# Column tiles of a projection in pairs by seven half-size products, in a hybrid attention block on one Trainium2 core

## The chip, the cores and the metric

The kernel runs on one core of a Trainium2 chip. The metric is device time in microseconds (us) of one launch. TensorE (PE) multiplies, VectorE (DVE) and ScalarE (ACT) work elementwise, GpSimd (POOL) fills, issues DMAs and does small things, SyncE (SP) issues the loads. Each engine works through its own queue in a fixed order and waits there on semaphores.

## The reference

One layer on 512 tokens of width 2048, in float32:

```python
h = rms_norm(x, pre_norm_w)
proj = h @ w_in   # sb_q | sb_k | sb_v | sb_gate | mla_c_q | mla_c_kv | mla_k_rope | mla_gate
...
y = concat(o_A * silu(sb_gate), o_B * silu(mla_gate)) @ w_out
return x + rms_norm(y, post_norm_w)
```

o_A is stick-breaking attention: 8 heads of 128, with weights sigmoid(z) times the running product of 1 - sigmoid(z) over the later keys. o_B is latent attention: 8 heads with low-rank queries and keys, a rotary part and a softmax.

## The kernel before, in words

**Numbers in two parts.** Every float32 operand is kept as a high and a low part in the type float32r (split, L94): ScalarE writes the rounded high part, VectorE the rest. One product is three matmuls (mm3, L127): high by high, high by low, low by high.

**Tiles.** hh and hl hold h transposed: 16 tiles of [128 columns of the model, 512 tokens]. column_proj (L217) makes one tile of 128 projected columns, [column, token]: two loads of weights of 512 KB each (weights, L104: one [128, 1024] tile raw, its parts whi and wlo), and for each 8 products on 512 tokens, 48 matmuls in all, in one PSUM bank. sb_queries (L360) and sb_keys (L367) make a head's q and k so, gate (L339) a head's gate; the per-token factor rstd_bc comes in afterwards. group_proj (L189) makes the values, four heads at a time, token by column.

**Order.** TensorE runs what is traced, in that order. The projections stand in a generator, filler (L449), that yields after each product; fill(n) (L467) takes n of its steps and stands between the parts of attention, so that TensorE has work while the other engines do softmax or scans. The filler makes the latents, eight gates, and then for every stick-breaking head its q, k and gate, with the values of four heads ahead of heads 0 and 4; then the output projection. The other engines' queues are ordered by the framework's scheduler; loads go out from SP in the order of the program.

**A stick-breaking head** (L733 to L760): four blocks of scores z, each masked on VectorE, two sigmoids on ScalarE (keep and beta), a scan (prod) and a product on VectorE; then, for each block of keys, transposes tp, their parts th and tl, and a product av with the values (Weighted, L576). The result is multiplied with the gate (mix) and put aside in memory.

**Buffers.** The pool ring holds raw in N_RAW = 2 slots and whi and wlo in N_HI = 3 each. A tile that takes a slot again waits until the last reader of the tile before it is done. One pool, gen, holds everything else for the whole run.

Of the kernel before, what the change touches and what calls it, by code (L numbers as in the profile page):

```python
# [10 lines left out]
F32 = mybir.dt.float32  # L11
# [46 lines left out]
def block(ctx: ExitStack, tc: tile.TileContext, a: dict):  # L58
# [4 lines left out]
    gen = ctx.enter_context(tc.tile_pool(name="gen", bufs=1))  # L63
    dram = ctx.enter_context(tc.tile_pool(name="dram", bufs=1, space=bass.MemoryType.DRAM))
# [4 lines left out]
    def g(name, dt=F32, tag="g"):  # L69
        return gen.tile([P, S], dt, tag=tag, name=name, bufs=SLOTS[tag])  # L70

# [40 lines left out]
    def small_weights(src, n, pin=False):  # L112
        raw = ring.tile([P, 768], F32, tag="mraw", name="mraw", bufs=1)
# [6 lines left out]
    # TensorE runs what is traced, in that order: the order below keeps it fed.  # L120
# [31 lines left out]
    def rms_factor(name, ss, n, cols):  # L152
        """(ss / n + eps) ** -0.5"""
# [6 lines left out]
    # TensorE's clock rises while it works  # L160
# [11 lines left out]
    def load_h(k, cuts=(slice(0, S),)):  # L172
        xk = g(f"xt{k}")
        hi, lo = g(f"hh{k}", F32R), g(f"hl{k}", F32R)
# [42 lines left out]
    def column_proj(t, out):  # L217
        """One tile of 128 columns, transposed: [column, token]; yields after each product."""
# [33 lines left out]
    def turns(n, unit, name):  # L252
        """fraction of a turn in n * unit radians, n a whole number of at most 12 bits"""
# [34 lines left out]
    # [block, half, 32]: cosines twice; sines with the sign of their half; the queries' ones scaled  # L288
    tabs = {}
    for nm, s in (("k", 1.0), ("q", MLA_SCALE)):  # L290
        ct = const.tile([P, NB, 2, 32], F32, name="cos_" + nm)
        st = const.tile([P, NB, 2, 32], F32, name="sin_" + nm)
# [19 lines left out]
    def latent(banks, n, width, name):  # L312
        """The scaled projection, token-major, and the sums of squares of its first n columns."""
# [35 lines left out]

    def sb_values(grp):  # L350
        banks = [bank(f"v{grp}_{b}") for b in range(NB)]
        yield from group_proj(a["w_v"][grp], S, banks)
        out = []
        for b in range(NB):
            hi, lo = g(f"vh{grp}_{b}", F32R), g(f"vl{grp}_{b}", F32R)
            split(hi, lo, banks[b], scale=rstd[:, b:b + 1])
            out.append((hi, lo))
        return out

    def sb_queries(h):  # L360
        ps = bank("qp")
        yield from column_proj(h * 3, ps)
# [495 lines left out]
```

## Time and profile before

| what | us |
|---|---|
| runs | 859.22, 858.12, 859.08 |
| median | 859.08 |
| span of the profiled execution | 857.2 |
| TensorE busy | 844.1 |
| VectorE busy | 425.0 |
| ScalarE busy | 337.8 |
| GpSimd busy | 42.1 |

The profiled execution has no time of its own in the record: its span, from the first to the last instruction, stands 1.9 us under the median of the runs, which has the start and the end of the launch in it. A busy TensorE is one with a matmul in flight; neighbouring matmuls overlap, so their pace is read from the chain, where a run of matmuls has a length and a count. Releasers are inferred from semaphore events.

### The profile page before, as it was taken

What the parts mean: (1) busy time and instruction counts of PE and PEld (TensorE: products, weight loads), DVE (VectorE), ACT (ScalarE), POOL (GpSimd) and SP (SyncE); (2) the same over time, 40 slices, a digit from 0 to 9 for tenths busy, and PEclk for the clock granted to TensorE, in tenths of its full rate; (3) what the DMA queues carried; (4) which work ended last, traced back from release to release, by engine and by line L of the source; (5) the groups of instructions that cost most, each with busy time, mean ns of one, the idle gap of its engine ahead of it and who ended that gap; (6) DMA issues with size and microseconds to landing.
All of it is one profiled execution on the core that took longest, in us unless ns stands there. A gap on an engine that the chain in (4) does not pass through costs nothing.

```text
span 857.2 us, 10780 instructions
## 1 busy us (share of the span) xinstructions
PE 844.1 (98%) x4146; PEld 711.9 (83%) x4146; DVE 425.0 (50%) x757; ACT 337.8 (39%) x585; POOL 42.1 (5%) x100
## 2 busy tenths in 40 slices
PE   8999999999999999999999999999999999999995
PEld 5889988888888888888888888888888888888885
DVE  5576755556556433536354524446364623244333
ACT  6743655554454423424243314323243423134201
POOL 1010000000000110000000000000001000000001
PEclk9999999999999999999999999999999999999998
DMA  9823222222221252222222224222223232336364
GB/s 314 317 75 101 99 86 75 81 93 80 93 81 62 76 192 97 79 100 85 97 88 86 89 96 135 99 86 95 89 81 132 97 110 99 111 103 204 112 190 153
DMA packets 32627, 97.19 MB, mean 113 GB/s; under 512 B 4144, under 2 KB 4672, under 8 KB 32576
## 3 DMA queue, kind: packets, MB, share of 16 engines
q1 hardware_dynamic: 27792, 82.46, 28.5%
q0 software_dynamic: 3488, 12.08, 4.3%
q10 hardware_dynamic: 1296, 1.97, 0.7%
q8 instruction: 32, 0.52, 0.3%
q14 instruction: 19, 0.16, 0.1%
HBM read 88.37 MB, written 8.13 MB: 113 GB/s over the span
## 4 chain that ended last, share of the span: by engine, by line
PE 93%; DVE 3%; ACT 1%; DMA 1%; issue 0%; POOL 0%; DVEq 0%; SPq 0%; ACTq 0%; POOLq 0%
PE y L122 20%; PE gps L122 19%; PE qp L122 10%; PE v L122 10%; PE kp L122 10%; PE cq L122 4%; PE av L122 4%; PE mz L122 3%; PE mqp L122 3%; PE ckv L122 2%; PE tp L125 2%; PE z L122 2%; PE qrp L122 1%; PE mv L122 1%; PE mkp L122 1%; DMA raw<-in_w_cq 1%
## 5 line engine op out<-in xcount | busy, mean ns | idle before, releaser
L99 DVE TENSOR_TENSOR wlo<-raw,whi 128x1024 fp32r<-128x1024 f32 (+2 forms) x124 | 147.5, 1190 | 187.8 <-ACT whi L96 186.0
L96 ACT CAST whi<-raw 128x1024 fp32r<-128x1024 f32 (+2 forms) x124 | 127.0, 1024 | 251.5 <-PE y L122 58.4
L122 PE MATMUL gps<-hh,whi 128*128 128x512 f32 x256 | 102.0, 398 | 0.0
L122 PE MATMUL gps<-hl,whi 128*128 128x512 f32 x256 | 100.1, 391 | 0.0
L122 PE MATMUL gps<-hh,wlo 128*128 128x512 f32 x256 | 99.9, 390 | 0.0
L122 PE MATMUL y<-whi,mxh 128*128 128x512 f32 (+1 forms) x222 | 85.5, 385 | 0.0
L122 PE MATMUL y<-whi,mxl 128*128 128x512 f32 (+1 forms) x222 | 85.1, 383 | 0.0
L122 PE MATMUL y<-wlo,mxh 128*128 128x512 f32 (+1 forms) x222 | 85.1, 383 | 0.0
L122 PEld LDWEIGHTS gps<-hh,wlo 128*128 128x128 f32 x256 | 48.1, 188 | 10.6
L122 PEld LDWEIGHTS gps<-hl,whi 128*128 128x128 f32 x256 | 48.2, 188 | 7.6
L122 PEld LDWEIGHTS gps<-hh,whi 128*128 128x128 f32 x256 | 48.2, 188 | 7.5
L122 PE MATMUL qp<-hh,whi 128*128 128x512 f32 x128 | 52.0, 407 | 0.0
L96 ACT CAST th<-tp 128x512 fp32r<-128x512 f32 (+1 forms) x64 | 27.1, 423 | 63.2 <-PE tp L125 63.2
L99 DVE TENSOR_TENSOR tl<-tp,th 128x512 fp32r<-128x512 f32 (+1 forms) x64 | 31.2, 488 | 39.9 <-ACT th L96 39.5
L122 PE MATMUL v<-whi,hh 128*128 128x512 f32 x128 | 50.9, 397 | 0.0
L122 PE MATMUL qp<-hh,wlo 128*128 128x512 f32 x128 | 50.1, 391 | 0.0
L122 PE MATMUL qp<-hl,whi 128*128 128x512 f32 x128 | 50.0, 391 | 0.0
L122 PE MATMUL v<-whi,hl 128*128 128x512 f32 x128 | 49.9, 390 | 0.0
L122 PE MATMUL v<-wlo,hh 128*128 128x512 f32 x128 | 49.9, 390 | 0.0
L122 PE MATMUL kp<-hh,whi 128*128 128x512 f32 x128 | 49.8, 389 | 0.0
L122 PE MATMUL kp<-hl,whi 128*128 128x512 f32 x128 | 49.8, 389 | 0.0
L122 PE MATMUL kp<-hh,wlo 128*128 128x512 f32 x128 | 49.8, 389 | 0.0
(246 smaller groups left out, 1618.5 us busy)
## 6 DMA issues: line engine op xcount, KB each, us to landing
raw<-in_w_t SPq DMA_DIRECT2D x64, 512.0 KB, 3.2
raw<-in_w_o SPq DMA_DIRECT2D x32, 512.0 KB, 3.2
raw<-in_w_v SPq DMA_DIRECT2D x16, 512.0 KB, 3.2
xs<-in_x SPq DMA_DIRECT2D x16, 256.0 KB, 6.2
xr<-in_x SPq DMA_DIRECT2D x16, 256.0 KB, 4.9
xt<-in_xt SPq DMA_DIRECT2D x15, 256.0 KB, 5.7
mixed<-mix POOLq DMA_DIRECT2D x15, 256.0 KB, 2.3
mx<-mixed POOLq DMA_DIRECT2D x15, 256.0 KB, 3.4
```

The lines of the kernel that those rows point to most:

```text
L96: i = act.copy(out=hi, in_=src)
L99: dve.tensor_tensor(out=lo, in0=src, in1=hi.bitcast(F32), op=ALU.subtract)
L122: tc.keep_in_program_order(pe.matmul(out=out, lhsT=lhsT, rhs=rhs, start=start, stop=stop, **kw))
L125: tc.keep_in_program_order(pe.transpose(out, in_, identity))
```

## The change

The two tiles of a pair (a head's q and k; the gates of two heads) are the columns of a product of two 2 x 2 block matrices: weights split by tile and by halves of the model's columns, h by halves of the model's columns and of the tokens. Strassen's scheme (in Winograd's form) makes such a product by seven products of blocks for eight. pair_proj does it, with each product 8 tiles of [128, 128] weights on 256 tokens, three matmuls each, so 24 matmuls of 256 columns:

1. A11: b1 (first tile, first half) by h's first block; 2. S1: b2 - b1 (b2 is the second tile, first half); 3. S2: b4 - (b2 - b1); 4. A12: b3 (first tile, second half); 5. S3: b4 - b2; 6. S4: b4 (second tile, second half); 7. A22: b3 - (b4 - b2 + b1).

The differences of weights are made in place by VectorE and split as before. For b1, b3 and b4 themselves the low part is made without VectorE: ScalarE writes the negated rounded value to wlo, and a DMA from POOL's queue adds the weights from memory to it. The sums of h's blocks are made once, from x reloaded: first_sums and last_sum, while TensorE makes the values, all of which now come ahead of the heads (those of the second four are put aside in memory and reloaded at head 4). VectorE puts the products together.

The pools follow the phases (PARTS), raw has four slots, and a step of a half product counts 0.53 of a step in fill. The filler's pairs stand in the order q and k of head 0, gates 0 and 1, q and k of heads 1 and 2, gates 2 and 3, and so on; the attention of head h stands between the matmuls of the pair that follows its own q and k, the last head's in the output projection.

```diff
-SLOTS = {"g": 46, "q4": 4, "row": 6, "tr": 4, "t": 4, "gt": 2, "mv": 4, "qrt": 8}
-N_RAW = 2
+
+SLOTS = {"q4": 4, "row": 6, "tr": 4, "t": 4, "gt": 3}
+PARTS = {
+    "h": {"h": 32},
+    "first": {"g1": 14, "mv": 4, "qrt": 8},
+    "values": {"v": 8},
+    "sums": {"s": 24},
+    "last": {"mx": 32, "mv3": 4, "w3": 16, "x3": 6},
+}
+N_RAW = 4
...
+    def first_sums(j):
+
+        x = ring.tile([P, 1024], F32, tag="raw", name="sx", bufs=N_RAW)
+        t = ring.tile([P, 1024], F32, tag="raw", name="st", bufs=N_RAW)
+        for i, k in enumerate((j, j + 8)):
+            c = slice(i * S, (i + 1) * S)
+            load(out=x[:, c], in_=a["xt"][k])
+            act.activation(out=x[:, c], in_=x[:, c], func=AF.Copy, scale=pre_w[:, k:k + 1])
+        a11, a21, a12, a22 = (x[:, i * HALF:(i + 1) * HALF] for i in range(4))
+        s1, s2, s4 = (t[:, i * HALF:(i + 1) * HALF] for i in range(3))
+        dve.tensor_tensor(out=s1, in0=a21, in1=a22, op=ALU.add)
+        dve.tensor_tensor(out=s2, in0=s1, in1=a11, op=ALU.subtract)
+        dve.tensor_tensor(out=s4, in0=a12, in1=s2, op=ALU.subtract)
+        h12, l12, hl4 = g("s12h", F32R, "s"), g("s12l", F32R, "s"), g("s4", F32R, "s")
+        split(h12, l12, t[:, :S])
+        split(hl4[:, :HALF], hl4[:, HALF:], s4)
+        sums[j] = h12, l12, hl4
...
+    def last_sum(j):
+
+        x = ring.tile([P, 1024], F32, tag="raw", name="sx", bufs=N_RAW)
+        load(out=x[:, :S], in_=a["xt"][j])
+        act.activation(out=x[:, :S], in_=x[:, :S], func=AF.Copy, scale=pre_w[:, j:j + 1])
+        s3 = x[:, S:S + HALF]
+        dve.tensor_tensor(out=s3, in0=x[:, :HALF], in1=x[:, HALF:S], op=ALU.subtract)
+        split(hh[j][:, HALF:], hl[j][:, HALF:], s3)
...
+        def parts(raw, src=None):
+            hi = ring.tile([P, 1024], F32R, tag="whi", name="whi", bufs=N_HI)
+            lo = ring.tile([P, 1024], F32R, tag="wlo", name="wlo", bufs=N_HI)
+            if src is None:
+                split(hi, lo, raw)
+            else:
+
+                act.activation(out=lo, in_=raw, func=AF.Copy, scale=-1.0)
+                pool.dma_start(out=lo, in_=src, accum_op=ALU.add)
+                act.copy(out=hi, in_=raw)
+            return hi, lo
...
+        def product(ps, w, which, start, stop):
+            for j, (ah, al) in enumerate(side(which)):
+                c = slice(j * P, (j + 1) * P)
+                mm3(ps[:, :HALF], w[0][:, c], w[1][:, c], ah, al, start and j == 0, stop and j == 7, skip_group_check=True)
+                yield 0.53
...
+        b1 = quarter(t1, 0)
+        w = parts(b1, a["w_t"][t1, 0])
+        yield from product(x, w, "A11", True, False)
+        act.copy(out=s1, in_=x[:, :HALF])
+        b2 = quarter(t2, 0)
+        sub(b1, b2, b1)
+        yield from product(z, parts(b1), "S1", True, True)
+        dve.tensor_tensor(out=s15, in0=z[:, :HALF], in1=s1, op=ALU.add)
+        b4 = quarter(t2, 1)
+        sub(b1, b4, b1)
+        yield from product(y, parts(b1), "S2", True, True)
+        dve.tensor_tensor(out=f.rearrange("p (i n) -> p i n", i=2), in0=y[:, :HALF].unsqueeze(1).broadcast_to([P, 2, HALF]),
+                          in1=e.rearrange("p (i n) -> p i n", i=2), op=ALU.add)
+        b3 = quarter(t1, 1)
+        w = parts(b3, a["w_t"][t1, 1])
+        yield from product(x, w, "A12", False, True)
+        sub(b2, b4, b2)
+        z = bank("sz")
+        yield from product(z, parts(b2), "S3", True, False)
+        dve.tensor_tensor(out=second[:, HALF:], in0=z[:, :HALF], in1=u4, op=ALU.add)
+        y = bank("sy")
+        yield from product(y, parts(b4, a["w_t"][t2, 1]), "S4", True, True)
+        dve.tensor_tensor(out=second[:, :HALF], in0=y[:, :HALF], in1=u4, op=ALU.add)
+        sub(b1, b3, b1)
+        yield from product(z, parts(b1), "A22", False, True)
+        dve.tensor_tensor(out=first[:, HALF:], in0=z[:, :HALF], in1=u2, op=ALU.add)
+        return x, first, second
...
+    def sb_pair(h):
+
+        x, q, kr = yield from pair_proj(h * 3, h * 3 + 1)
+        act.copy(out=q[:, :HALF], in_=x[:, :HALF])
         qh, ql = g("qh", F32R, "q4"), g("ql", F32R, "q4")
-        split(qh, ql, ps)
-        return qh, ql
-
-    def sb_keys(h):
-        ps = bank("kp")
-        yield from column_proj(h * 3 + 1, ps)
-        kr = g("kr", tag="tr")
-        dve.tensor_tensor(out=kr, in0=ps, in1=rstd_bc, op=ALU.mult)
+        split(qh, ql, q)
+        dve.tensor_tensor(out=kr, in0=kr, in1=rstd_bc, op=ALU.mult)
         kh, kl = g("kh", F32R, "q4"), g("kl", F32R, "q4")
         split(kh, kl, kr)
-        return kh, kl
-
-    # chunks of the output projection: the latent heads' first
+        done["q", h], done["k", h] = (qh, ql), (kh, kl)
...
+        for grp in range(2):
+            yield from sb_values(grp)
+        done["values",] = True
         for h in range(H):
-            if h % 4 == 0:
-                done["v", h // 4] = yield from sb_values(h // 4)
-            done["q", h] = yield from sb_queries(h)
-            done["k", h] = yield from sb_keys(h)
-            done["gate", h] = yield from gate(h * 3 + 2, "gt")
+            yield from sb_pair(h)
+            if h % 2 == 0:
+                yield from gate_pair(h)
+        close_part("sums")
+        close_part("h")
+        open_part("last", "right")
...
+        due[0] += n
         taken[0] += n
+        while due[0] > 0:
+            due[0] -= next(steps, None) or 1
...
+    close_part("first")
+    open_part("sums", "right")
+    open_part("values", "left")
+    for j in range(8):
+        first_sums(j)
+        fill(8 if j < 7 else 5)
+    done["v", 0] = split_values(done["v", 0], [rstd[:, b:b + 1] for b in range(NB)])
+    for j in range(8):
+        fill(4)
+        last_sum(j)
+    while ("values",) not in done:
+        fill(1)
...
+        if h == H // 2:
+            done["v", 1] = late_values()
+        cur = Weighted(rows, done["v", h // 4], (h % 4) * P)
```

How this orders the engines is seen at three places; what stands in brackets is what the row waits for (an engine, or a queue of loads: DMAHW for SP's, DMASW for POOL's).

**Place 1: ScalarE's queue where a head's attention ends.** Before, at the end of head 1's scores: z, keep and beta are the scores, th the parts of the transposed rows, whi the weights' casts.

```order
L96 CAST whi_3713<-raw_3711 128x1024 [waits DMAHW5_49,PE_49]
L346 ACTIVATE sg_3594<-gt_3592 128x512 [waits DVE_49,Activation_49]
L96 CAST th_3618<-tp_3613 128x512 [waits PE_49]
L96 CAST th_3639<-tp_3635 128x384 [waits PE_49,Pool_49]
L96 CAST whi_3743<-raw_3741 128x1024 [waits DMAHW6_49,PE_49]
L96 CAST th_3664<-tp_3661 128x256 [waits DVE_49,PE_49]
L96 CAST th_3682<-tp_3680 128x128 [waits DVE_49,PE_49]
L96 CAST whi_3780<-raw_3778 128x1024 [waits DMAHW7_49,PE_49]
L96 CAST qh_3706<-qp_3597 128x512 [waits PE_49]
```

Now, head 0's attention beside the pair of gates 0 and 1. raw_4144 is that pair's b4 and raw_4044 its b1, which by now holds the difference for A22; raw_4368 is b1 of the next pair.

```order
L926 ACTIVATE beta_4088<-z_4169,rq_pos_585 128x512
L463 ACTIVATE wlo_4260<-raw_4144 128x1024 [waits DMASW5_49,PE_49]
L116 CAST whi_4312<-raw_4044 128x1024 [waits PE_49]
L116 CAST th_4238<-tp_4233 128x512 [waits PE_49]
L465 CAST whi_4370<-raw_4368 128x1024 [waits DMAHW5_49,PE_49,Activation_49]
L463 ACTIVATE wlo_4371<-raw_4368 128x1024 [waits DMASW6_49,PE_49]
L116 CAST th_4275<-tp_4271 128x384 [waits PE_49,Pool_49]
L116 CAST th_4300<-tp_4297 128x256 [waits DVE_49,PE_49]
```

Ahead of th for the second block of keys there now stand a cast that waits for a load of SP's queue (DMAHW5) and a negation, both for the next pair; before, the cast there waited for TensorE alone. The same order stands at the seven places where a pair's end carries attention.

VectorE's queue at the same place; raw_4406 and raw_4438 are the next pair's b2 and b4.

```order
L119 TENSOR_TENSOR wlo_4313<-raw_4044,whi_4312 128x1024 [waits DMASW7_49,DMASW0_49,Activation_49]
L119 TENSOR_TENSOR tl_4239<-tp_4233,th_4238 128x512 [waits Activation_49]
L501 TENSOR_TENSOR c2_4043<-sz_4219,f_4041 128x256 [waits DVE_49,PE_49]
L475 TENSOR_TENSOR raw_4368<-raw_4406,raw_4368 128x1024 [waits DMAHW6_49,DMAHW5_49,Activation_49]
L119 TENSOR_TENSOR tl_4276<-tp_4271,th_4275 128x384 [waits Activation_49]
L475 TENSOR_TENSOR raw_4406<-raw_4438,raw_4406 128x1024 [waits DMAHW7_49,DVE_49]
L119 TENSOR_TENSOR tl_4301<-tp_4297,th_4300 128x256 [waits Activation_49]
```

The next pair's first two differences, which wait for its loads and its negation, stand ahead of tl for the second and third block.

**Place 2: ScalarE's queue where a pair without attention beside it ends** (q and k of head 1; raw_4368 is its b1, raw_4438 its b4, raw_4610 the next pair's b1).

```order
L116 CAST whi_4503<-raw_4406 128x1024 [waits PE_49]
L465 CAST whi_4533<-raw_4438 128x1024 [waits DMAHW7_49,DVE_49,PE_49]
L463 ACTIVATE wlo_4534<-raw_4438 128x1024 [waits DMASW0_49,PE_49]
L116 CAST whi_4564<-raw_4368 128x1024 [waits DVE_49,PE_49,Activation_49]
L465 CAST whi_4612<-raw_4610 128x1024 [waits DMAHW1_49,DVE_49,PE_49]
L513 COPY c1_4366<-sx_4361 128x256 [waits DMASW4_49]
L463 ACTIVATE wlo_4613<-raw_4610 128x1024 [waits DMASW1_49,PE_49]
```

A22's cast waits for TensorE and for the difference; then the next pair's cast for its load, and the negation, after which POOL's queue issues the adding DMA.

**Place 3: VectorE's queue at the turn from the pair of head 2 to that of gates 2 and 3** (ql and kl are the low parts of head 2's q and k, mix the result of head 1, raw_4935 b1 of the next pair).

```order
L507 TENSOR_TENSOR c1_4608<-sz_4785,f_4607 128x256 [waits PE_49]
L769 TENSOR_TENSOR mix_4954<-av_4836,gt_4357 128x512 [waits PE_49]
L119 TENSOR_TENSOR wlo_5034<-raw_4935,whi_5033 128x1024 [waits Activation_49]
L119 TENSOR_TENSOR ql_4920<-c1_4608,qh_4919 128x512 [waits Activation_49]
L475 TENSOR_TENSOR raw_4935<-raw_5084,raw_4935 128x1024 [waits DMAHW0_49,DVE_49]
L119 TENSOR_TENSOR kl_4925<-c2_4609,kh_4924 128x512 [waits Activation_49]
```

kl, which the scores of head 2 need, stands behind mix, a low part for the next pair and one of its differences.

## Rows read from the trace of the kernel before

**Rows 1.** The page's busy table: engine, busy us, share of the span, instructions.
```profile
PE 844.1 (98%) x4146; PEld 711.9 (83%) x4146; DVE 425.0 (50%) x757; ACT 337.8 (39%) x585; POOL 42.1 (5%) x100
```
**Rows 2.** The chain that ended last: shares of the span by engine, by line.
```profile
PE 93%; DVE 3%; ACT 1%; DMA 1%; issue 0%; POOL 0%; DVEq 0%; SPq 0%; ACTq 0%; POOLq 0%
...
PE y L122 20%; PE gps L122 19%; PE qp L122 10%; PE v L122 10%; PE kp L122 10%; PE cq L122 4%; PE av L122 4%; PE mz L122 3%; PE mqp L122 3%; PE ckv L122 2%; PE tp L125 2%; PE z L122 2%; PE qrp L122 1%; PE mv L122 1%; PE mkp L122 1%; DMA raw<-in_w_cq 1%
```
**Rows 3.** TensorE's waits: engine, line, released by, us in total, times, longest.
```profile
PE mz L122 <- ACT p L662: 0.7, 1, 0.7
...
PE av L122 <- DVE tl L99: 0.2, 1, 0.2
```
**Rows 4.** Busy times in one head's stretch: PE, PEld, DVE, ACT, POOL, clock, DMA.
```profile
376.00:413.80 37.80, 37.80 (x180) 31.62 (x179) 19.05 (x29) 13.17 (x22) 0.95 (x3) 1.00 0.27 91
```
**Rows 5.** The chain in order of time: start us, us, what.
```profile
69.16 5.76 PE qrp L122 x48
...
95.46 0.89 PE rb_ps L122 x8
...
338.27 10.88 PE kp L122 x48
```
**Rows 6.** VectorE's groups by form: busy us, mean ns of one, idle before.
```profile
L99 DVE TENSOR_TENSOR wlo<-raw,whi 128x1024 fp32r<-128x1024 f32 x114 | 139.6, 1224 | 181.4 <-ACT whi L96 179.6 <-PE av L122 1.1
...
L99 DVE TENSOR_TENSOR tl<-tp,th 128x384 fp32r<-128x384 f32 x16 | 8.9, 558 | 24.4 <-ACT th L96 24.4
...
L747 DVE TENSOR_TENSOR_SCAN prod<-keep,zero 128x512 f32<-128x512 f32 x8 | 9.8, 1225 | 5.7 <-ACT keep L745 5.7
...
L603 DVE TENSOR_TENSOR mix<-av,gt 128x512 f32<-128x512 f32 x8 | 5.5, 692 | 14.1 <-PE av L122 14.1
...
L371 DVE TENSOR_TENSOR kr<-kp,rstd_bc 128x512 f32<-128x512 f32 x8 | 5.5, 692 | 26.6 <-PE kp L122 26.6
...
L506 DVE TENSOR_TENSOR qru<-qru 128x256 f32<-128x256 f32 x8 | 3.4, 420 | 0.0
```
**Rows 7.** ScalarE's groups by form, as before.
```profile
L96 ACT CAST whi<-raw 128x1024 fp32r<-128x1024 f32 x114 | 119.9, 1052 | 231.3 <-PE y L122 58.4 <-PE kp L122 42.6 <-PE v L122 38.1
...
L101 ACT ACTIVATE hh<-xt,pre_w 128x512 fp32r<-128x512 f32 x15 | 10.2, 715 | 1.2 <-DMA xt<-in_xt 1.0
...
L96 ACT CAST th<-tp 128x256 fp32r<-128x256 f32 x16 | 5.9, 368 | 4.3 <-PE tp L125 4.3
...
L745 ACT ACTIVATE keep<-z,rq_neg 128x512 f32<-128x512 f32 x8 | 5.5, 690 | 11.7 <-DVE z L743 11.7
...
L101 ACT ACTIVATE vh<-v,rstd 128x512 fp32r<-128x512 f32 x8 | 5.5, 688 | 4.7 <-PE v L122 4.7
```
**Rows 8.** Busy times early on, columns of rows 4; last DMA share, GB/s.
```profile
8.00:13.50 5.50, 4.22 (x16) 2.55 (x14) 3.39 (x6) 4.08 (x6) 0.00 (x0) 1.00 1.02 403
```
**Rows 9.** Waits of SP's queue, as in rows 3.
```profile
SPq L88 <- DVE wlo L99: 484.8, 91, 11.6
```
**Rows 10.** Timeline of ScalarE and VectorE, 380 to 386 us: start, us, what.
```profile
381.34 1.05 ACT L96 CAST whi<-raw 128x1024 fp32r<-128x1024 f32 x1 [3.96 <-issue]
...
382.43 1.22 DVE L99 TENSOR_TENSOR wlo<-raw,whi 128x1024 fp32r<-128x1024 f32 x1 [3.67 <-ACT whi L96]
```
**Rows 11.** DMA issues: issuing queue, count, KB each, median us to landing.
```profile
raw<-in_w_t SPq DMA_DIRECT2D x64, 512.0 KB, 3.2
...
mraw<-in_w_head POOLq DMA_DIRECT2D x8, 384.0 KB, 3.3
...
mraw<-in_w_kvv POOLq DMA_DIRECT2D x4, 256.0 KB, 2.8
```
**Rows 12.** Timeline of TensorE, 0 to 8 us: the warm-up.
```profile
1.26 4.28 PE L122 MATMUL warm_ps<-idle 128*128 128x512 bf16 x10 [1.26 <-DVE idle L162]
```

More of the change, by code (lines that the diff above doesn't have):

```diff
@@ L67, in block, with g @@
     psum = ctx.enter_context(tc.tile_pool(name="psum", bufs=4, space=PSUM))
-    def g(name, dt=F32, tag="g"):
-        return gen.tile([P, S], dt, tag=tag, name=name, bufs=SLOTS[tag])
+    open_part("h", "right")
+    open_part("first", "left")
+    def g(name, dt=F32, tag="g1"):
+        home, n = homes[tag]
+        return home.tile([P, S], dt, tag=tag, name=name, bufs=n)
     def bank(name, dt=F32):
@@ L112, in small_weights @@
     def small_weights(src, n, pin=False):
+        ring = pools["first"]
         raw = ring.tile([P, 768], F32, tag="mraw", name="mraw", bufs=1)
@@ L348, in gate, with split_values @@
         return gr
+    aside = [dram.tile([P, S], F32, name=f"values{b}") for b in range(NB)]
+    def split_values(srcs, scale=None):
+        out = []
+        for b in range(NB):
+            hi, lo = g("vh", F32R, "v"), g("vl", F32R, "v")
+            split(hi, lo, srcs[b], scale=scale and scale[b])
+            out.append((hi, lo))
+        return out
     def sb_values(grp):
@@ L352, in sb_values @@
         yield from group_proj(a["w_v"][grp], S, banks)
-        out = []
+        if grp == 0:
+            done["v", 0] = banks
+            return
         for b in range(NB):
[L355 to L362, printed above, removed]
-        qh, ql = g("qh", F32R, "q4"), g("ql", F32R, "q4")
-        split(qh, ql, ps)
-        return qh, ql
@@ new lines, in block @@
+    HALF = S // 2
+    sums = {}
+    def first_sums(j):
[14 more added lines that the diff above has]
+        sums[j] = h12, l12, hl4
@@ new lines, in last_sum, with side @@
+    def last_sum(j):
[5 more added lines that the diff above has]
+        split(hh[j][:, HALF:], hl[j][:, HALF:], s3)
+    def side(which):
+        lo_, hi_ = slice(0, HALF), slice(HALF, S)
+        if which == "A11":
+            return [(hh[j][:, lo_], hl[j][:, lo_]) for j in range(8)]
+        if which == "A12":
+            return [(hh[j + 8][:, lo_], hl[j + 8][:, lo_]) for j in range(8)]
+        if which == "A22":
+            return [(hh[j + 8][:, hi_], hl[j + 8][:, hi_]) for j in range(8)]
+        if which == "S1":
+            return [(sums[j][0][:, lo_], sums[j][1][:, lo_]) for j in range(8)]
+        if which == "S2":
+            return [(sums[j][0][:, hi_], sums[j][1][:, hi_]) for j in range(8)]
+        if which == "S3":
+            return [(hh[j][:, hi_], hl[j][:, hi_]) for j in range(8)]
+        return [(sums[j][2][:, lo_], sums[j][2][:, hi_]) for j in range(8)]
@@ new lines, in pair_proj, with quarter, sub @@
+    def pair_proj(t1, t2):
+        def quarter(t, half):
+            raw = ring.tile([P, 1024], F32, tag="raw", name="raw", bufs=N_RAW)
+            load(out=raw, in_=a["w_t"][t, half])
+            return raw
+        def parts(raw, src=None):
[13 more added lines that the diff above has]
+                yield 0.53
+        def sub(out, x, y):
+            dve.tensor_tensor(out=out, in0=x, in1=y, op=ALU.subtract)
+        x, z, y = bank("sx"), bank("sz"), bank("sy")
+        e, f = g("e", tag="tr"), g("f", tag="tr")
+        s1, s15, u2, u4 = e[:, :HALF], e[:, HALF:], f[:, :HALF], f[:, HALF:]
+        first, second = g("c1", tag="tr"), g("c2", tag="tr")
+        b1 = quarter(t1, 0)
[25 more added lines that the diff above has]
+        return x, first, second
@@ L416, in post_weight @@
         return pw
[L418 removed]
+    w_tags = iter(["t"] * 4 + ["w3"] * 16)
     ws = []
@@ L465, in block @@
     taken = [0]
+    due = [0.0]
     def fill(n):
-        for _ in range(n):
-            next(steps, None)
+        due[0] += n
         taken[0] += n
+        while due[0] > 0:
+            due[0] -= next(steps, None) or 1
     def need(*key):
@@ L803, in block @@
             at += w
+    for part in list(pools)[::-1]:
+        close_part(part)
 def _layout(x, positions, pre_norm_w, w_in, q_norm_w, w_q_up, kv_norm_w, w_kv_up, w_out, post_norm_w):
```

48 lines of the change are left out of this document (37 added, 11 removed).

## Prediction, made before the changed kernel ran

> **What bounds the kernel now.** I read the busy table first: TensorE is busy 844.1 us of a span of 857.2, VectorE half of it, ScalarE 39% [rows 1]. The chain that ended last says that this is no accident of overlap: 93% of the span is TensorE, and qp, kp and gps, the tiles that the change touches, are among its largest parts [rows 2]. Then the table of waits, TensorE alone: after the start it waits for 0.7 us here and 0.2 us there, so nothing that the other engines do is late [rows 3]. One head of the stick-breaking stage takes 37.80 us with TensorE busy for all of it, VectorE for 19.05 and ScalarE for 13.17 [rows 4]. So TensorE's issue rate sets the time, a saving there counts in full, and any wait that the change brings to TensorE counts in full too. The profiled execution spans 857.2 us; the median of the three runs is 859.08, so 1.9 us lie around the span.
>
> **What the seven products save.** A column tile is 48 matmuls of 512 columns in 10.88 us, 226.7 ns each; 48 matmuls of 256 columns in a row take 5.76 us, 120.0 ns each [rows 5]. So the half width costs 6% per column, weight loads included. A pair is 2 x 10.88 = 21.76 us before, and 7 x 8 x 3 = 168 matmuls x 0.120 = 20.16 us after: 1.60 us a pair, **19.2 us for the 12 pairs**. The values' 384 matmuls are only done earlier. The Trainium skill (TensorE: Matmul & The Clock Gate, Back-to-back issue gap) gives columns / 2.4 GHz plus 2.5 ns. By it a pair would go from 20.7 to 18.3 us and the twelve would save 28 us; the rows are slower at both widths, and their 19.2 stands.
>
> **What is added beside TensorE.** Per pair VectorE makes four differences and four low parts of 1024 (1.22 each), five combinations (0.42 or 0.69), ScalarE seven casts (1.05) and three negations [rows 6, 7]. A scaled copy of 512 takes 0.715, so a negation of 1024 lies between 1.05 and 1.43; I take 1.15. Over two heads (three pairs) that is, with attention's share of rows 4, some 60 us of VectorE and 48 us of ScalarE beside 3 x 20.16 + 2 x 5.16 = 70.8 us of TensorE. No engine is overfull; 36 adding DMAs of 512 KB and the reloads add some 27 MB to 97, and the queues have moved 403 GB/s [rows 8]. **So only latency and order within the queues can cost time, and they do**, for two reasons that the code fixes. With N_HI = 3, the high and low part of the seventh product (A22) go into the buffers of the fourth (A12), so its cast cannot start before the fourth product has ended; call that T. And b1 of the next pair is loaded into the slot of this pair's b1, which A22's low part reads last. Today's loads are held in the same way, 91 times, by the low part [rows 9], but there the next weights are two tiles of work away; here three products of 2.88 us are left.
>
> The chain from T: 0.2 until the cast starts, cast 1.05, low part 1.22 (it starts 1.09 after the cast [rows 10]), load issued at T+2.6, landed 3.2 later [rows 11] at T+5.8.
>
> **Term A, pairs whose end carries a head's attention (7).** The ACT rows in the section on the change put the next pair's cast and negation, which wait for that load, ahead of th for the second block of keys, and the DVE rows put the next pair's first difference, which waits for the negation, ahead of tl. So: cast to T+6.85, negation to T+8.0, difference to T+9.2, tl (0.56) to T+9.8 [rows 6, 7]. TensorE arrives at the product that needs tl after the fifth product (2.88), seven transposes of 0.11 [rows 5], one product of 0.68 with the first block, and 18 to 24 matmuls of the sixth: T+6.5 for gates 0 and 1, T+6.8 for head 6, T+7.2 for five. The waits: 3.3 + 3.0 + 5 x 2.6 = **19.3 us**. The adding DMA of the next pair is hidden under them, since TensorE then needs the new product only after a further 4.8 us.
>
> **Term B, pairs whose end carries no attention and that another pair follows (heads 0, 1, 3, 5).** Cast to T+6.85, a copy of 256 (0.37 [rows 7]), negation to T+8.35, then the adding DMA, X, against TensorE's arrival at T + 3 x 2.88 + 0.24 = 8.9. The trace has no adding DMA. Lower bound: a plain load of 512 KB, 3.2; upper: twice a POOL load of that size, which by the 2.8 for 256 and 3.3 for 384 KB is 3.8, so 7.6 [rows 11]. I take X = 4.8: nearest are POOL's own loads, 3.8, and the old values have to be read too. The wait is 8.35 + 4.8 - 8.9 = 4.25 each, **17.0 us** (10.6 to 28.2). The Trainium skill (Collectives: The Full Stack, The bandwidth ceiling) says that an add in a DMA costs not its arithmetic but a second read on the same ring, which halves the rate. By that only the moving part of 3.8 doubles, an estimate of X = 5.8 and 4 us more in this term; no run here shows it yet.
>
> **Term C, A12 in the five pairs with bare TensorE (heads 0, 1, 3, 5, 7).** Its buffers are those of the first product: 0.2 + 1.05 + 1.15 + X = 7.2 after that product's end, with two products, 5.76, in between: 1.4 each, 7.2 us (0 to 21); in the first pair four copies of the values (0.69 each [rows 7]) stand ahead, 1.4 more. **8.6 us.** S4 has the same chain, but A12's wait covers it.
>
> **Term D, keys of heads 2, 4, 6.** After the last av, VectorE does mix 0.69, a low part 1.22, ql 0.69, a difference 1.22 and kl 0.69, 4.7 us with the hand-over, and TensorE has 15 + 6 matmuls, 2.5 us, before the first score: 3 x 2.2 = **6.6 us**.
>
> **Edits costed at nothing.** The sums of x: their chain is load, two scaled copies, three sums, two casts, two low parts, about 9 us with four slots, beside 68 us of value products (300 matmuls) with three weight pieces ahead. The last scores to the first transpose: mask, sigmoid 0.69, scan 1.22, product 0.69 and what stands between is 4.7 to 5.3 us [rows 6, 7] against 4.7 us of matmuls; if that cover goes it is 0.5 x 7 us. The reloaded values have three blocks' time, and the output projection's first weights come at about the last product's end.
>
> **Sum.** 857.2 - 19.2 + 19.3 + 17.0 + 8.6 + 6.6 = 889.5 of span, and with 1.9 around it **891 us**, 3.8% slower than before. With X at 3.2 it is 876, with X at 7.6 it is 918.
>
> **Rivals.** *The buffers do not hold A22 (faster).* The order shows that A22's cast waits for TensorE, not for which matmul. If the wait were for a product two or more earlier, the chain would start 5.8 us sooner, terms A to C would be gone, and of the rest D alone would stay, perhaps 4: 859.1 - 19.2 + 4 = **844 us**. It decides from a chain that starts 4.3 us sooner. For it: TensorE waits nowhere today [rows 3] although the same three buffers serve it. Against: three buffers and seven products leave no other slot. Chance 0.14.
> *The waits are half covered*, by work that I have put too early or by loads that land sooner: half of 51.5 us stays, 866 us, down to no change. Chance 0.07.
> *The adding DMA runs at half a load's speed or worse*, X from 6 to 7.6 and over: 903 to 918. For it: nothing in this trace adds in flight. Chance 0.11.
> *TensorE's clock falls in the new waits.* Every stretch reads a clock of 1.00 now, but the ten warm-up matmuls, after idleness, take 4.28 us, 0.43 each [rows 12], about the pace of 1.2 GHz where 0.227 is that of 2.4; ten matmuls at that pace lose 2.0 us. If each of the 11 waits of A and B is followed by such a stretch it is 22 us, **913 us**. Against: the waits of A and B are 3 to 4 us in over 20 of work. The Trainium skill (TensorE: Matmul & The Clock Gate, Why this matters for your kernels) asks that TensorE have no long idle gaps between bursts, for this reason; whether these are long enough no row of before shows. Chance 0.11.
> *The change does not do what it says*: the halves could cost TensorE more than 0.120 each. The row is 48 in a line with a new weight load each, the pattern of the products, so I give it no more than the 0.02 that is left.
>
> **Chances.** The forecast (870 to 903 us) has 0.55, the others as above: 0.55 + 0.14 + 0.07 + 0.11 + 0.11 + 0.02 = 1. A measurement of this kernel can tell some 0.2%, 1.7 us, from no change. Faster: 0.14. The same: 0.03, out of the half-covered case. Slower: the rest, 0.83. For 8 times in 10 the range leaves out most of the fast rival and the slowest tail of the two slow ones: **855 to 922 us**.
>
> **What would show each step.** Right: matmuls of 256 columns 120 ns apart; TensorE waiting in seven places for tl before av on 384 columns, about 3 us each; in four places for a low part that the adding DMA brings (4 us); ScalarE idle for some 3 us ahead of a cast that the load of b1 releases; adding DMAs landing in about 4.8 us. Wrong: TensorE without such waits; a load of b1 issued well before T+2.6, T being the end of the fourth product; adding DMAs under 3.2 or over 7.6 us; a granted clock below 1 in the stage, which would move the cause from the queues to the clock.

## The result, and the profile after

The changed kernel takes **952.03 us** (median of 4 runs, 948.52 to 954.37) where the kernel before, run beside it, takes 858.94: a ratio of **1.108** (95% interval 1.105 to 1.111). The forecast was 891, range 855 to 922: slower, as forecast, but by 93 us and not by 32. The profiled execution spans 952.6 us.

The page's busy table, chain shares and DMA issues of the kernel after answer to [rows 1, 2, 11]:

```profile
PE 865.4 (91%) x5010; PEld 760.4 (80%) x5010; DVE 526.3 (55%) x925; ACT 441.0 (46%) x729; POOL 77.5 (8%) x144
...
PE 67%; DMA 14%; issue 10%; DVE 6%; ACT 3%; POOL 0%; SPq 0%; DVEq 0%; POOLq 0%; ACTq 0%
...
raw<-in_w_t SPq DMA_DIRECT2D x64, 512.0 KB, 4.1
wlo<-in_w_t POOLq DMA_DIRECT2D x36, 512.0 KB, 7.0
```

TensorE's waits, to be held against [rows 3], where no tile of a head's q, k or gate waited:

```profile
PE sy L143 <- DMA wlo<-in_w_t: 30.1, 8, 5.6
PE sx L143 <- DMA wlo<-in_w_t: 27.9, 11, 4.9
PE y L143 <- ACT whi L116: 4.1, 1, 4.1
PE z L143 <- ACT beta L926: 2.6, 2, 1.9
PE z L143 <- ACT kh L116: 2.5, 3, 0.8
PE z L143 <- DVE kl L119: 1.7, 3, 0.6
...
PE av L143 <- DVE tl L119: 0.8, 1, 0.8
```

The whole stage of the pairs, in the columns of [rows 4]:

```profile
381.65:749.50 367.85, 304.89 (x2251) 295.27 (x2251) 217.14 (x316) 175.97 (x250) 40.65 (x63) 0.90 0.53 130
```

Two things are new. TensorE stands still: 87.2 us of the span (952.6 - 865.4) against 13.1 before, and 58.0 of the 74.1 us more wait for the adding DMA, at the low part of A11 and A12 (sx) and of S4 (sy). And while it works it works more slowly: its busy time rose by 21.3 us although it has less to do, and the granted clock in the stage is 0.90, so part of the stage ran at 1.2 GHz and not at 2.4. The chain in order of time shows both at one A12 of a pair without attention:

```profile
381.65 2.85 PE sx L143 x24
...
395.26 5.06 PE sx L143 x22
```

A11 takes 2.85 us for 24 matmuls; A12, after a wait, takes 5.06 us for its last 22. The timelines of ScalarE, GpSimd (POOL) and TensorE tell where that wait came from (start, us, what, in brackets the idle time before):

```profile
384.45 1.05 ACT L465 CAST whi<-raw 128x1024 fp32r<-128x1024 f32 x1 [1.14 <-issue]
385.40 0.37 ACT L485 COPY e<-sx 128x256 f32<-128x256 f32 x1
385.67 1.06 ACT L463 ACTIVATE wlo<-raw 128x1024 fp32r<-128x1024 f32 x1
```
```profile
387.03 0.90 POOL L464 DMA_DIRECT2D wlo<-in_w_t  x1 [3.43 <-ACT wlo L463]
```
```profile
395.26 0.58 PE L143 MATMUL sx<-hh,wlo 128*128 128x256 f32 x1 [4.86 <-DMA wlo<-in_w_t]
```

A11 ends at 384.3 and frees the buffer. The negation starts 1.35 later, behind the cast of A12's own high part and the copy of A11's sum; the DMA is issued at 387.03, and TensorE goes on at 395.26, 8.2 us after the issue. The two products in between took 5.7.

S4 waits in the pairs that carry attention, and for one reason more. In the first pair of gates S2 ends at 422.3 and frees S4's buffer:

```profile
422.43 1.05 ACT L465 CAST whi<-raw 128x1024 fp32r<-128x1024 f32 x1 [1.73 <-issue]
423.38 0.69 ACT L925 ACTIVATE keep<-z,rq_neg 128x512 f32<-128x512 f32 x1
423.96 0.68 ACT L926 ACTIVATE beta<-z,rq_pos 128x512 f32<-128x512 f32 x1
424.53 1.06 ACT L463 ACTIVATE wlo<-raw 128x1024 fp32r<-128x1024 f32 x1
```
```profile
425.89 0.86 POOL L464 DMA_DIRECT2D wlo<-in_w_t  x1 [9.54 <-ACT wlo L463]
```
```profile
434.07 0.58 PE L143 MATMUL sy<-s,wlo 128*128 128x256 f32 x1 [5.17 <-DMA wlo<-in_w_t]
```

The negation stands on ScalarE behind the cast and the two sigmoids of the last scores, 2.2 us after its buffer was free, and then come 8.2 us of DMA again.

A11 waits for the same reason, and not for the load of its weights b1. Of the pair of gates behind head 0, b1 was issued at 386.75, while A12 of head 0 ended at 400.0:

```profile
386.75 0.33 SPq L108 DMA_DIRECT2D raw<-in_w_t  x1
```

What comes late is the buffer of the low part, which is that of S3, two products earlier. S3's matmuls end at 403.06, and the chain goes on with cast, copy, negation and DMA:

```profile
403.09 1.05 ACT whi L465
404.14 0.27 ACT c L513
404.41 0.97 ACT wlo L463
405.37 0.28 issue
405.66 5.25 DMA wlo<-in_w_t
```

### The profile page after: what moved, and what is told of

The parts are those of the page before. It is cut to its first block, busy times and chain, and to the rows that moved or that the text cites. A ratio compares the mean times of both kernels' runs of the same rounds, so it can differ in the third digit from the quotient of the medians.

```text
span 952.6 us, 13072 instructions
## 1 busy us (share of the span) xinstructions
PE 865.4 (91%) x5010; PEld 760.4 (80%) x5010; DVE 526.3 (55%) x925; ACT 441.0 (46%) x729; POOL 77.5 (8%) x144
## 4 chain that ended last, share of the span: by engine, by line
PE 67%; DMA 14%; issue 10%; DVE 6%; ACT 3%; POOL 0%; SPq 0%; DVEq 0%; POOLq 0%; ACTq 0%
PE y L143 17%; DMA wlo<-in_w_t 12%; PE gps L143 9%; PE v L143 9%; PE sx L143 6%; PE sz L143 4%; PE cq L143 4%; PE av L143 3%; PE mz L143 3%; PE sy L143 3%; PE mqp L143 2%; PE ckv L143 2%; PE tp L146 1%; PE qrp L143 1%; PE mv L143 1%
## 5 line engine op out<-in xcount | busy, mean ns | idle before, releaser
L143 PE MATMUL y<-whi,mxh 128*128 128x512 f32 (+1 forms) x222 | 87.2, 393 | 4.1 <-ACT whi L116 4.1
L143 PE MATMUL sx<-hh,wlo 128*128 128x256 f32 x192 | 61.4, 320 | 27.9 <-DMA wlo<-in_w_t 27.9
L475 DVE TENSOR_TENSOR raw<-raw 128x1024 f32<-128x1024 f32 x48 | 58.5, 1220 | 20.5 <-ACT wlo L463 16.8
L143 PEld LDWEIGHTS sx<-hh,wlo 128*128 128x128 f32 x192 | 42.2, 220 | 30.2 <-DMA wlo<-in_w_t 30.1
L143 PE MATMUL sx<-hh,whi 128*128 128x256 f32 x192 | 59.2, 308 | 0.0
L143 PE MATMUL sx<-hl,whi 128*128 128x256 f32 x192 | 59.1, 308 | 0.0
L143 PE MATMUL sy<-s,wlo 128*128 128x256 f32 x96 | 31.1, 324 | 30.1 <-DMA wlo<-in_w_t 30.1
L143 PE MATMUL sz<-hh,whi 128*128 128x256 f32 x192 | 56.4, 294 | 0.0
L143 PE MATMUL sz<-hl,whi 128*128 128x256 f32 x192 | 54.5, 284 | 0.0
L143 PE MATMUL sz<-hh,wlo 128*128 128x256 f32 x192 | 54.4, 283 | 0.0
L143 PEld LDWEIGHTS y<-whi,mxh 128*128 128x128 f32 x222 | 41.9, 189 | 13.6 <-ACT whi L116 4.3
L143 PE MATMUL gps<-hh,whi 128*128 128x512 f32 x128 | 52.2, 408 | 0.0
```

The lines of the kernel that those rows point to most:

```text
L143: tc.keep_in_program_order(pe.matmul(out=out, lhsT=lhsT, rhs=rhs, start=start, stop=stop, **kw))
L475: dve.tensor_tensor(out=out, in0=x, in1=y, op=ALU.subtract)
```

## Experiments

Each ran with the kernel before on the same chip, whose medians lie between 858.77 and 859.19 us.

**1. Who makes the low part.** The first four take the adding DMA away, the addition alone, the shortage of buffers, and the standing still.

```diff
-                act.activation(out=lo, in_=raw, func=AF.Copy, scale=-1.0)
-                pool.dma_start(out=lo, in_=src, accum_op=ALU.add)
-                act.copy(out=hi, in_=raw)
+            split(hi, lo, raw)
```

> Low parts of b1, b3 and b4 by VectorE like the others, no negation and no adding DMA. Theory 1 (the adding DMA's 7.0 us from issue to landing do not fit into the two products that its buffer leaves, and each wait is followed by matmuls at half pace): the chain is cast 1.05 and low part 1.22, 2.5 us against 5.7, so the waits of sx and sy, 58 us now, fall under 10, the granted clock returns to 0.98 or more, and the time is 855 to 870. Rival (three buffers and the late load of b1 hold the products, whoever makes the low part): TensorE still waits 40 us or more, then for whi or wlo from ScalarE and VectorE, 910 to 940. Second rival (VectorE with 44 us more is late for attention): waits for tl, beta or kl of 3 us in seven places, 870 to 890.

**875.92 us**, ratio 1.019 (1.018 to 1.021). The waits of sx and sy are gone altogether, none is left in the list, and the clock is 0.991:

```profile
PE y L143 <- ACT whi L116: 4.2, 1, 4.2
PE tp L146 <- DVE beta L923: 3.0, 4, 0.8
PE av L143 <- DVE tl L119: 2.6, 4, 1.2
```
```profile
381.65:672.00 290.35, 279.53 (x2258) 271.84 (x2256) 252.81 (x351) 145.11 (x216) 10.98 (x30) 1.00 0.31 101
```

Theory 1 holds for the waits and the clock, and the first rival falls: three buffers and the load of b1 are enough when the low part is not brought by a DMA. The time lies 6 us over the theory's range and inside that of the second rival, but the waits that this one asked for, some 3 us in seven places, are not there: for beta, tl and kl TensorE waits 9.5 us in all, 1.8 at the longest. 76 of the 93 us were this one step. The 6 us led to experiments 5, 9 and 13.

```diff
-                pool.dma_start(out=lo, in_=src, accum_op=ALU.add)
+                pool.dma_start(out=lo, in_=src)
```

> The same DMA without the addition: the buffer is overwritten with the weights, so the low part is left out of three of seven products. Theory 1a (the adding itself is slow): issue to landing falls from 7.0 to 4 to 4.5 us, A12 and S4 still wait some 0.5 us each, the time is 870 to 890. Theory 1b (any DMA issued by POOL in this stage takes as long, since it shares the engines with SP's loads): landing stays at 6 us or more, the time within 15 us of 952.

**891.67 us**, just over the range of theory 1a; 19.3 us of waiting are left (11.2 for sy, 8.1 for sx). The DMA row:

```profile
wlo<-in_w_t POOLq DMA_DIRECT2D x36, 512.0 KB, 4.3
```

So the same transfer from the same queue, in the same place, takes 4.3 us plain and 7.0 adding: the addition is 2.7 us of it, and costs 60 us of the kernel. The Trainium skill (Collectives: The Full Stack, The bandwidth ceiling) puts the price of an add in a DMA down to a second read, at half the rate; the two rows agree with the direction, 1.6 times as long.

> Four buffers for low parts in the pairs' stage, the room made by leaving out the operand S4 (the product uses S1's tile in its place). Theory 1: a negation may start one product (2.85 us) earlier; 19 waits of 58 us in all lose up to 2.85 us each, about 12 to 20 us stay, the matmuls at half pace go with them, 870 to 895. Rival (the DMAs are limited by what the queues carry; an earlier start only makes more of them overlap): landing grows from 7 to 9 us or more, waits of 40 us and over, 925 or more.

The edit takes the low parts from a pool of their own, `pools["sums"].tile(..., tag="plo", bufs=4)`. **896.23 us**, again just over the range. 13.5 us of waiting are left, and landing stays at 7.0, so the rival falls: it was the lead of two products against a latency, not what the queues can carry. A buffer more and a DMA without the addition give about the same.

```diff
...
+                if j == 0 and idle:
+                    db = bank("dummy")
+                    for _ in range(idle):
+                        mm(db[:, :HALF], w[0][:, c], ah, True, True)
+                mm(ps[:, :HALF], w[1][:, c], ah, False, stop and j == 7, skip_group_check=True)
...
```

> Nothing is taken away; where A12 (heads 0, 1, 3, 5, 7) and S4 (the other seven pairs) wait for their first low part, TensorE runs 24 or 20 matmuls of 256 columns whose result nobody reads (2.85 and 2.4 us). Theory of the clock (the pace of 0.21 us a matmul after a wait, against 0.119, comes from TensorE having stood still): the matmuls behind the shortened waits run at 0.119, some 2.2 us less in each of 12 places, and the time falls to 915 to 935 though work is added. Rival (the slow matmuls come from something else, such as the DMA writing their weights): 948 to 965, and 0.21 after each wait as before.

**947.63 us**, 4.4 less with 31 us of work more (260 matmuls at 0.119); the intervals of the two ratios just touch. The theory was right on the pace and wrong on the time. The chain of this kernel at the A12 of head 1:

```profile
447.32 6.87 DMA wlo<-in_w_t
454.19 0.04 issue
454.24 2.86 PE sx L143 x22
```

Behind a filled wait the 22 matmuls take 2.86 us, where they took 5.06 behind an empty one; the mean clock rose from 0.955 to 0.977. But sx still waits 21.5 us: at the five filled A12 it is 5.8 where it was 18.3, but at A11 9.8 where it was 7.2, and at A12 of the pairs of gates 5.9 where it was 2.4. TensorE that is faster only comes earlier to the next adding DMA. The slow clock was real, and mostly paid by time that would have been waited anyway.

**2. The cheap ways out.**

```diff
-        sub(b1, b3, b1)
-        yield from product(z, parts(b1), "A22", False, True)
+        sub(b3, b3, b1)
+        yield from product(z, parts(b3), "A22", False, True)
```

> The difference for A22 is written over b3 and not over b1, so that b1's buffer is free for the next pair's load when the difference is made, not when A22's low part is. Theory of the forecast (the late load of b1 is half of the trouble): the 8 us of A11's waits go and with them the matmuls at half pace there, 930 to 942. Rival (the adding DMA and its buffer hold A11, A12 and S4; the load of b1 would have come in time): 945 to 953.

**935.18 us**, 17 less and in the theory's range, but not for the theory's reason. sx waits 14.6 us where it waited 27.9, sy 32.4 for 30.1; of sx, A11 lost 3.0 us (7.2 to 4.2) and A12 10.3 (20.7 to 10.4). And the load of b1 was not late to begin with: in the change it is issued 6.4 to 13.3 us before A12 ends, with this edit 6.7 to 8.7. What changed is the landing of the adding DMA:

```profile
wlo<-in_w_t POOLq DMA_DIRECT2D x36, 512.0 KB, 6.0
```

In the change six adding DMAs of A12 are issued 0.2 to 0.5 us behind the load of the next pair's b1, and they land after 6.6 to 8.2 us; five are issued 1.0 us or more ahead of it, and they land after 5.4 to 5.9. With the edit all eleven are ahead of it, and eight of them land after 5.2 to 5.8, three after 6.1 to 7.2. So the edit seems to work by which of the two DMAs goes first. No run tests that alone, and in the change with padding (experiment 10) both kinds land after 6.0 to 7.0. The rival's account, that the adding DMA and its buffer hold all three products and b1 comes in time, is what the traces show; its time is wrong.

> In each product the 16 matmuls with the high part of the weights run first and the 8 with the low part last, so TensorE needs the low part 1.66 us later; adding DMAs stay. Theory 1 (each wait stands alone): 19 waits lose up to 1.66 us each, 25 us and more, with the half pace behind the short ones, 905 to 925. Rival (the waits form a loop of buffer, negation and adding DMA; TensorE that comes sooner waits at the next place, as the filled waits showed): 935 to 952.

The edit runs the loop over the eight steps twice, first the two matmuls with the high part, then the one with the low part. **912.39 us** (ratio 1.061, 1.056 to 1.066), as theory 1 has it: 40 us for an order of matmuls. Waits for the adding DMA fall from 58.0 to 20.9. The rival, which the filled waits had suggested, falls: a longer lead helps at every wait, idle work hardly.

> Each adding DMA of 512 KB in two of 256 KB, one behind the other on the same queue; the first four steps of a product need only the first. Theory A (its time goes with the bytes): a half lands 4 to 5 us after its issue, TensorE's waits shrink by 2 us each, 905 to 930. Theory B (its time is mostly a fixed latency): halves land after 6 us or more and the time stays over 940.

**924.65 us**, theory A on time; on the latency both were off. The row of both halves together:

```profile
wlo<-in_w_t POOLq DMA_DIRECT2D x72, 256.0 KB, 6.0
```

The first halves land 5.3 us after their issue in the median, the second ones, which stand behind them in the queue, 6.8. The two together are there 7.3 us after the first issue, no sooner than one whole DMA; TensorE gains because it can begin with the first half.

**3. What the rest costs.**

> The control: queries, keys and gates by two whole column tiles as before, while everything else of the change stays (values first and reloaded, the sums of x made though not used, pools by phase). Theory 1 (all that the change costs is in the products and what feeds them, but for some 10 us between the last product and the output projection): 866 to 873. Rival (the new order and the phases cost more by themselves): 880 or more. It prices the rest of the change, against which the products by seven have to be measured.

In `sb_pair` and `gate_pair` the call of `pair_proj` gives way to two of `column_proj`. **889.54 us**: the rival, and far more than the gap that I knew of. No wait over 3.5 us stands in the list; the chain has the cause, beside [rows 5]:

```profile
381.95 11.20 PE qp L143 x48
```

A column tile takes 11.20 us and not 10.88, at a clock of 1.00. So it is from the first product on, in code that the change leaves alone: TensorE's busy time is 865.0, 20.9 more than before. What differs is where the tiles lie. The program's allocation has the tiles of x at 2016 over a multiple of 2048 bytes, before at 768.

```diff
+    for side_ in ("right", "left"):
+        pad = tc.alloc_tile_pool(name="pad_" + side_, bufs=1, side=side_)
+        pad.tile([P, 8], F32, name="pad_" + side_)
...
```

> The control of whole column tiles again, with 32 bytes put ahead of the pools of each side. In the program of the change the tiles of x, of its sums and of the mixed heads begin 32 bytes off a multiple of 64, in the kernel before on a multiple of 64 (768 over a multiple of 2048); in the control a matmul of 512 columns takes 0.2333 us where before it took 0.2267, from the first product on, in code that the change leaves alone. Theory (the place of the tiles sets the pace): 0.2267 again, some 3000 matmuls by 6.6 ns, 20 us less, 867 to 872. Rival (the pace comes from something else in the program): 0.2333 and 888 to 891 as without.

**884.75 us**, 4.8 less and not 20: the projections that have x as the stationary operand went from 0.2333 to 0.2289 us a matmul (by the distance of their starts), those that stream it stayed. A multiple of 64 was the wrong measure. With 56 in place of 8 numbers in the pad:

> The control of whole column tiles with 224 bytes ahead of the pools, so that every tile of 2 KB begins on a multiple of 256 bytes as in the kernel before (with 32 bytes the tiles of x and of the mixed heads stood at 192 over such a multiple). Theory of the place, sharpened (a moving operand or a weight load off a multiple of 256 is slower): 0.2267 us a matmul of 512 columns in all stages, 20 us less than the control without, 868 to 873. Rival (the place explains only the 4.8 us that the first padding gave, the rest is the program): 883 to 888.

**876.41 us**, and the pace of before is back in all stages:

```profile
378.41 10.88 PE qp L148 x48
```

The place is worth 13.1 us in the control. Of the other 17.6 over the kernel before, 11.9 are TensorE standing still (875.0 - 850.0 = 25.0 against 13.1), half of that where the output projection waits for the mixed heads and head 7's first scores; 5.9 are busy time, and 3.2 of it are matmuls at half pace in two stretches, behind the wait of the values at 309 us and that of the output projection.

> The change itself with the same 32 bytes. Theory of the place: some 1850 matmuls of 512 columns are 6.6 ns faster, 12 us, and the 2016 of 256 columns, 0.1185 now, may go back to the 0.120 of before, 3 us; 940 to 946. Rival (the pace is not from the place): 949 to 955.

**944.91 us** in the change itself, 7.1 less, the theory's time but not its parts: matmuls of 512 columns that stream x stayed at 0.233 us, and those of 256 columns went down, to 0.114 to 0.117, and not up to 0.120.

**4. All together.**

> Low parts by VectorE, A22's difference over b3, low products last, the first two tiles of the mixed heads loaded ahead of the last product, the first casts of the output projection in a fixed order, two products more ahead of the scores of heads 2, 4 and 6. Theory 1 (what is left over 859 in the run with VectorE's low parts is waits: 4.6 us for keys, 6.7 for beta, th and tl, 7 between the last product and the output projection): 858 to 867. Rival (what is left is TensorE's own pace, 15 us of busy time over the count of matmuls): 870 to 876.

**867.88 us**, 0.9 over theory 1's range.

> The kernel of all the edits together, aligned in the same way, and with only the first cast of the output projection's weights and of the mixed heads in a fixed order. Theory of the place: 9 us less than the 867.9 of the version without, and 1 to 2 us from the order: 855 to 860, as fast as before or a little faster. Rival: 866 to 869.

**859.41 us**, ratio 1.000 (0.999 to 1.001), as the theory has it: level with the kernel before.

> The version of all the edits with 32 bytes of padding, with 192 more ahead of the mixed heads' pool, and with six more products per head placed between the scores and ahead of the transposes. Theory (what is left are VectorE's late answers, 8 us for beta, kl and th, and 2 us of pace in the output projection): 848 to 855, faster than before. Rival (the products that are used earlier are missing at the head's end, so the waits only move): 857 to 861.

**864.50 us**: the theory falls, and the time is over the rival's range too. av waits 6.9 us for tl and 3.7 for th, where in the version before it waits 0.7 and 1.0: the waits moved, as the rival says. TensorE is also busy for 5.4 us more (831.5 against 826.1), at a mean clock of 0.984 against 0.996.

> As the one with more fill, and the low part of b3 (A12) made by GpSimd, which takes 15 us off VectorE. Theory (VectorE's load of 65% to 95% in the stage is what makes beta and kl late): 2 to 4 us less than with VectorE alone. Rival (GpSimd takes 3.5 us or more for 1024 numbers and slows VectorE while it runs, so A12 or VectorE waits instead): the same or up to 15 us more.

**874.51 us**: the theory falls again. GpSimd takes 2.58 us for a low part in the mean, and VectorE, 1.22 alone, takes 2.63 beside it here:

```profile
L465 POOL TENSOR_TENSOR wlo<-raw,whi 128x1024 fp32r<-128x1024 f32 x12 | 30.9, 2578 | 111.1 <-DVE wlo L465 57.8 <-DVE raw L481 20.7 <-PE tp L151 20.7
```
```profile
503.63 2.63 DVE L465 TENSOR_TENSOR wlo<-raw,whi 128x1024 fp32r<-128x1024 f32 x1
```

The Trainium skill (GPSIMD Engine Reference, Specifications) says that GpSimd shares its way to the buffers with VectorE, with contention where an instruction has two inputs there; these rows agree in part: of five instructions of VectorE on two inputs of 1024 that fell on one of GpSimd's for 1 us or more, two took 2.63 us and one 3.40, but two took 1.22 as alone.

> The version of all the edits with 32 bytes of padding and the old number of products between the scores; 192 bytes more ahead of the mixed heads' pool; and the first weights of the output projection are cast before the last product ends, the first two tiles of the mixed heads ahead of the last queries and keys. Theory (the 3.2 us of waiting behind the last product and the half pace behind it, 2 to 3 us, go, and 816 matmuls of the output projection at 0.2267 instead of 0.2289 give 1.8): 852 to 856, faster than before by 0.3 to 0.8%. Rival (the wait goes over to the second weights or to the keys of head 7): 857 to 860.

**852.96 us**, ratio **0.992** (0.991 to 0.994): below both kernels, by 0.8% of the kernel before, which is clear of the noise and small. Of the 4.9 us that y waited 0.6 are left, and TensorE is busy for 824.8 us:

```profile
PE 824.8 (97%) x5010; PEld 728.7 (86%) x5010; DVE 561.2 (66%) x961; ACT 407.2 (48%) x693; POOL 44.8 (5%) x106
```

## Why the prediction was wrong

**The account.** Between the two profiles lie 95.4 us; the forecast put 32.3 between them. What each step cost, in us:

| step | forecast | measured |
|---|---|---|
| the halves: a product takes 2.85, a pair 7 x 2.85 = 19.95 against 21.76 | -19.2 | -21.7 |
| A: waits for tl in the seven pairs with attention | 19.3 | 0 |
| B: A11 behind the four bare pairs | 17.0 | 7.2 |
| C: A12 in the five bare pairs | 8.6 | 18.3 |
| A12 in pairs with attention | 0 | 2.4 |
| S4 | 0 | 30.1 |
| D: keys of heads 2, 4 and 6 | 6.6 | 4.2 |
| matmuls at half pace | 0 | 30.7 |
| matmuls of 512 columns, some 1600, slower by up to 6.6 ns (an estimate) | 0 | 10 |
| the start of the output projection | 0 | 6.8 |
| the rest | 0 | 7.4 |

The half pace is half of the 61.5 us for which TensorE was busy while the granted clock was 0.5. The waits and the pace of single matmuls are read from the trace, wait by wait.

**Right.** The bound (TensorE), that every wait counts in full, the saving, and one of the two causes: an adding DMA against the time of two products. With it gone the waits are gone (experiment 1).

**Term C, A12, and X.** The first step that failed is "I take X = 4.8: nearest are POOL's own loads". X is 7.0 in the median (5.3 to 8.8) and 8.2 in the A12 shown; the upper bound, 7.6, was nearer than the value taken. The rest of this chain was right: 2.4 us from the free buffer to the issue were forecast, 2.7 came.

**"S4 has the same chain, but A12's wait covers it."** This is the largest single error among the waits, 30.1 us costed at nothing. In the bare pairs it is nearly true, 1.6 us in all. But I used it for all twelve, and in the seven with attention A12 hardly waits, the scores cover it; S4 has no such cover, and its negation stands behind the sigmoids.

**Terms A and B, "load issued at T+2.6".** This chain was not there. The prediction has b1 of the next pair loaded into the slot of this pair's b1. In the program it takes the slot of this pair's b3, which is free as soon as A22's difference and A12's negation are made; it is the next pair's b3 that takes b1's slot and is issued behind A22's low part, 2.4 to 3.5 us after T. The load of b1 is issued 6.4 to 13.3 us before T in all eleven turns and has landed before T. So the sign that I had named for being wrong, a load of b1 well before T+2.6, came. No product in the seven pairs waits for tl; the 0.8 us in the list are head 7's, in the output projection. A11 does wait, in the places of term B, but for the adding DMA behind S3's buffer, as shown above. These two terms put 29 us too much into the sum, which hid as much of what was missing: that the forecast came within 61 us is luck.

**Term D** has the right cause, 4.2 us (kh and kl) for 6.6.

**The clock** was a rival of its own, 0.11, at 2 us for each of 11 waits. It came true beside the forecast, not in place of it: 30.7 us, of them 3 behind waits that no adding DMA made. I should have added it to the cases with waits. It is not 31 us that can be had back, as the filled waits show.

**At nothing.** "The output projection's first weights come at about the last product's end": the weights did, the mixed heads did not, since their room is free only when x is read for the last time. 4.9 us at y and 1.9 more at the scores behind it. And I took the paces of the unchanged code over from the kernel before; the pools by phase moved the tiles, about 10 us. The same move made the halves cheaper than their row, 2.85 us a product for 2.88.

**The range** took in X up to 7.6 with everything else as forecast (by its own terms that is 916 us and not 918). Of the two slow rivals, the adding DMA and the clock, each was priced as if the other did not come; with S4 beside them the time lies 30 us beyond the range.

## What to carry to other kernels

Saving 2.5% of TensorE's time is worth having only when the operands come as fast as before: count for each one the latency from its buffer's release to its arrival, against the products in between, and put nothing with a DMA in that chain if an engine with time left can do it. Before a chain is built on a buffer's release, look up in the program which tile had that slot. Waits that come behind one another are not covered by the first in those stretches where the first has other cover; check each kind of stretch. After a move of pools compare the pace of matmuls that nobody touched.

## What was not expected of the hardware

- The place of an operand sets TensorE's pace. 512 columns take 0.2267 us with all tiles on multiples of 256 bytes (10.88 for 48) and 0.2333 with x and the mixed heads 32 bytes off a multiple of 64. With these at 192 over a multiple of 256 they take 0.2289 where x or the mixed heads are the stationary operand, and still 0.2333 where x is the one that streams. With 256 columns it is the other way round: 48 matmuls take 5.75 us with all on multiples of 256, 5.68 with the streamed operand at 32 over one, and 5.44 and 5.65 with it at 64 (the rows of qrp). The products of a pair take 2.85 us for 24 with x 32 bytes off a multiple of 64, and 2.72 in the last version, with x at 192. Why was not tested.
- A DMA that adds takes 7.0 us for 512 KB in the median, where a plain one from the same queue takes 4.3. Single ones land after 5.3 to 8.8: those for A11 after 5.8 in the median, those for S4 after 7.9. A11's have 1.9 us of SP's weight loads in flight beside them in the mean, S4's 8.4.
- Behind waits of 2.9 to 4.9 us TensorE ran the 22 matmuls of A11 or A12 in 5.06 or 5.07 us; behind waits of 1.9 and 2.1 in 2.90 and 2.87, but behind another of 1.9, at A12 of head 5, in 4.04. The length of the wait alone does not tell.
